# One 512-column matmul for the high and low part of the activations, with the sum of the two PSUM halves at the evacuation

## The chip, the cores and the metric

The kernel runs on one core of one Trainium2 chip. The metric is the device time of one execution, in microseconds (us); smaller is better. TensorE is PE in the rows (its weight loads are PEld), VectorE is DVE, ScalarE is ACT, GpSimd is POOL, SyncE is SP.

## The reference

One layer of a decoder trunk on 256 tokens of width 2048. Cut to what matters here:

```python
proj = x @ w_in                      # 256 x 2048 by 2048 x 15392
# split of the columns: lru_x, lru_y, gla_q, gla_k, gla_v, gla_r, dn_qkv, beta, a, dn_z, gate_logits
y_lru = rg_lru(lru_x, lru_y)         # causal conv of 4 taps, gates, scan
y_gla = gla(gla_q, gla_k, gla_v, gla_r)
y_dn  = gated_deltanet(dn_qkv, beta, a, dn_z)      # causal conv of 4 taps, silu, chunk recurrence
gates = sigmoid(gate_logits + b_gate)
m = (gates[0] * (y_lru @ w_branch[0]) + gates[1] * (y_gla @ w_branch[1])
     + gates[2] * (y_dn @ w_branch[2])) @ w_out
x1 = layernorm(alpha * x + m)
out = layernorm(alpha * x1 + square(relu(x1 @ w1 + b1)) @ w2 + b2)   # hidden width 8192
```

All inputs are float32.

## The kernel before, in words

Each float32 operand of a large product is split into a high part (`hi`, the value as float32r) and a low part (`lo`, the rest), by `split` (L93): a cast on ACT (L94) and a subtraction on DVE (L95). A product is then three matmuls: hi by hi, hi by lo, lo by hi.

Most of the products are channel tiles: `jobB` (L129) computes 128 output channels for all 256 tokens. The weights are stationary (a 128 x 128 tile of `hi` or `lo` for each slice of 128 of the contraction), the activations move with 256 columns (`xh`, `xl`; in the MLP `x1h`, `x1l`). `mmB` (L121) takes 8 slices: for each of them weight `hi` by `xh` (L124) and the same weight `hi` by `xl` (L125), then eight times weight `lo` by `xh` (L127). All add up in the first 256 columns of one PSUM tile (`accB`, 512 columns wide, four buffers). A job of 16 slices is 48 matmuls. There are 113 channel tiles in the mixers (the first four run in a loop of their own, L187 to L191, slice by slice as x arrives) and 64 in the first product of the MLP (the first three in a loop of their own, L1089 to L1094, with the transposes of x1).

`evac` of the job then takes the PSUM tile: a causal conv (L343: a scaled copy on ACT, three multiply-adds of 253 to 255 columns on DVE that read PSUM), a plain copy (L362), products with decays (L422, L430, L431), a silu (L434), a tanh for a gate (L864), or in the MLP relu and square, both on ACT (L1037, L1038).

The other products have the weights as the moving operand: GLA's values (L467 to L469) and the output projection (L915 to L917) with 512 columns and, in one quarter, 256, the second product of the MLP (L1199 to L1201) with 512 and 256. The branch projections (`job_branch`, L975) have weights stationary and 256 columns moving, as a channel tile has, with `yh` and `yl`.

What sets the order: `run_jobs` (L1002) walks the list of jobs; before it emits the matmuls of a job, it emits the load (1 MB by SP's queue, three buffers) and the split of the job after it (`hi` and `lo` have three buffers of 8 slices each). After a job, `pump` (L145) emits steps of the mixers (LRU, GLA, DeltaNet), up to about 2 us of DVE and 2.2 us of ACT work, whose small matmuls stand between the jobs on PE. The order on each engine is then fixed by the scheduler when the program is built, by priority and data dependence; at run time each engine takes its instructions in this order.

Of the kernel before, what the change touches and what calls it, by code (L numbers as in the profile page):

```python
# [25 lines left out]
# columns of the packed per-channel parameters  # L26
# [16 lines left out]
# columns of the packed constants  # L43
# [10 lines left out]
# columns of the parameters that are needed later  # L54
# [4 lines left out]
# rows of the small projections in their channel tile  # L59
# [6 lines left out]
def trunk_kernel(ctx, tc, xw, xtok, par, lat, con, wab, wa2, wB, wV, wBr, wO, w1, w2a, w2b, rows, out):  # L66
# [23 lines left out]
    def t1_tile(name, shape, dt=F32):  # L90
        return sm.tile(shape, dt, tag="t1", name=name, bufs=6)
# [6 lines left out]
    xh = [big.tile([P, 8, T], F32R, tag="xh", name=f"xh{i}", bufs=2) for i in range(2)]  # L98
    xl = [big.tile([P, 8, T], F32R, tag="xl", name=f"xl{i}", bufs=2) for i in range(2)]
# [29 lines left out]
    def jobB(src, evac, rh=None, rl=None):  # L129
        rh, rl = rh or xh, rl or xl  # L130
        job = Job(src, 8 * len(rh), None, None)

        def mm():
            acc = mm_tile("accB")
            n = len(rh)
            for i in range(n):
                mmB(acc[:, :T], job, rh[i], rl[i], i, i == 0, i == n - 1)
            evac(acc[:, :T])
# [24 lines left out]
    # ---- inputs that the first jobs need  # L163
    # x and the first four channel tiles together, one slice of the contraction at a time
# [11 lines left out]
    for k in range(KT):  # L176
# [56 lines left out]
    # ---- small projections: GLA's low rank, beta and decay of DeltaNet  # L233
# [9 lines left out]
    def evac_small(acc):  # L243
        ve.tensor_scalar(zs, acc, col(C_DTB), col(C_SGN), ALU.add, ALU.mult)
        live.append(gen_small())

    def gen_small():
        # GLA's log decay: 16 gk per head
# [47 lines left out]
        # beta, g: token rows  # L296
# [19 lines left out]
        # GLA: cumulated log decay in chunks of 64, and its exponentials  # L316
# [23 lines left out]
    # ---- LRU  # L340
# [10 lines left out]
    def evac_lru_x(k):  # L351
        def f(acc):
            if k % 4 == 0:
                lru["xc", k // 4] = b4_tile("xc", [P, 4, T])
            conv(acc, lru["xc", k // 4][:, k % 4, :], C_LRU_W + 4 * k, col(C_LRU_B + k))
# [11 lines left out]
    def gen_lru(hf):  # L367
# [14 lines left out]
        # gelu  # L382
# [32 lines left out]
    # ---- GLA  # L415
    gla = {}

    def evac_gla_q(h):
        def f(acc):
            if h == 0:  # L420
                gla["qe"] = b4_tile("qe", [P, 4, T])
            ve.scalar_tensor_tensor(gla["qe"][:, h, :], acc, P ** -0.5, gla["eb"][:, h, :], ALU.mult, ALU.mult)  # L422
        return f

    def evac_gla_k(h):
        def f(acc):
# [7 lines left out]
    def silu2(acc, dst, use_act=True):  # L434
        """dst = 2 silu(acc)"""
# [4 lines left out]
    def evac_gla_r(k):  # L440
        def f(acc):
            if k % 4 == 0:
                gla["r", k // 4] = b4_tile("rr", [P, 4, T])
            silu2(acc, gla["r", k // 4][:, k % 4, :])
# [164 lines left out]
    def evac_dn_z(k):  # L609
        def f(acc):  # L610
            if k % 4 == 0:
                dn["z"][k // 4] = b4_tile("dz", [P, 4, T])
            silu2(acc, dn["z"][k // 4][:, k % 4, :])
# [31 lines left out]
    def gen_dn():  # L645
# [6 lines left out]
        for tt in range(NT):  # L652
# [31 lines left out]
            # inverse of the unit upper triangle I + M, blocks of 32 by substitution  # L684
# [37 lines left out]
            # blocks of 64, then of 128: D - D N D  # L722
# [45 lines left out]
            # chunk recurrence  # L768
# [88 lines left out]
    # ---- gates and branches  # L857
# [31 lines left out]
    # ---- output projection, first norm  # L889
# [112 lines left out]
    def run_jobs(js, hooks=()):  # L1002
        """Jobs in order; the split of a job stands before the mixers' steps of the one before it."""
# [23 lines left out]
    # ---- MLP, first product  # L1027
    x1h = [big.tile([P, 8, T], F32R, tag="xh", name=f"x1h{i}", bufs=2) for i in range(2)]
    x1l = [big.tile([P, 8, T], F32R, tag="xl", name=f"x1l{i}", bufs=2) for i in range(2)]
    h = []  # L1030

    def evac_h(c):
        def f(acc):
# [3 lines left out]
            sc.activation(t, acc, AF.Relu, bias=col(C_B1 + c))  # L1037
            sc.activation(h[c // 4][:, c % 4, :], t, AF.Square)  # L1038
# [3 lines left out]
    js = [jobB(w1[c], evac_h(c), x1h, x1l) for c in range(FF // P)]  # L1042
# [19 lines left out]
    # ---- norm of the mixer, transposed for the MLP  # L1062
    mv = [norm_stats(tt) for tt in range(NT)]
    acc = [mm_tile("accH") for _ in range(G)]
    for q in range(4):
# [6 lines left out]
        for kp in range(2):  # L1072
# [271 lines left out]
```

## Time and profile before

| | |
|---|---|
| Time, three runs | 1744.10, 1744.58, 1745.21 us |
| Median | 1744.58 us |
| Span of the profiled execution | 1743.0 us (the page gives no other time of it) |
| PE busy | 1722.7 us, 99% of the span |
| DVE busy | 1058.2 us, 61% |
| ACT busy | 889.8 us, 51% |
| POOL busy | 76.7 us, 4% |
| Granted clock of PE, mean over the run | 0.997 |

The span goes from the first to the last instruction of the one profiled execution; the runs are timed without it. The median lies 1.6 us above the span. A busy PE says that matmuls were under way, not that they started as closely as they can: what one costs in a stream is read from the starts of its neighbours, since the duration of one (283 ns for 256 columns) goes on while the next have begun.

### The profile page before, as it was taken

The page shows a single profiled execution, that of the slowest core. Times are in us where ns is not written, and L with a number is a line of the kernel's source. Part 1 is how long each engine was busy: PE and PEld are TensorE (multiplying, and loading weights), DVE is VectorE, ACT ScalarE, POOL GpSimd, SP SyncE. Part 2 cuts the span into 40 slices and gives each one's busy share as a digit, 9 for nine tenths or more (in the row PEclk, how much of TensorE's full clock was granted, in tenths as well). Part 3 has the DMA queues.
Part 4 walks back from the last instruction along what each step waited for, and adds up shares of the span by engine and source line. Part 5 has one row for each costly group of instructions (what it writes and reads, how often), then busy time and mean ns, then how long its engine had stood idle before and what let it go on. Part 6 is the DMA issues. An engine that isn't in the chain of part 4 may idle for free.

```text
span 1743.0 us, 30261 instructions
## 1 busy us (share of the span) xinstructions
PE 1722.7 (99%) x12782; PEld 1644.9 (94%) x12782; DVE 1058.2 (61%) x1353; ACT 889.8 (51%) x1209; POOL 76.7 (4%) x112
## 2 busy tenths in 40 slices
PE   8999999999999999999999999999999999999997
PEld 8999898999999999999998899999999988888897
DVE  7876456876765585565555675444444455576767
ACT  6785445785344443444444455554545444455553
POOL 0000000000120203000000000000000000000000
PEclk9999999999999999999999999999999999999999
DMA  8445543444564446355566835555545455555552
GB/s 328 150 170 187 197 173 125 166 170 149 184 194 148 161 170 187 130 181 182 184 217 223 308 109 209 190 177 187 187 177 193 172 192 195 194 193 193 203 193 97
DMA packets 52536, 319.96 MB, mean 184 GB/s; under 512 B 6752, under 2 KB 7136, under 8 KB 18992
## 3 DMA queue, kind: packets, MB, share of 16 engines
q1 hardware_dynamic: 49280, 310.92, 50.3%
q0 software_dynamic: 2976, 6.84, 1.5%
q8 instruction: 100, 1.64, 0.4%
q14 instruction: 36, 0.29, 0.0%
q10 hardware_dynamic: 144, 0.26, 0.0%
HBM read 315.09 MB, written 2.88 MB: 182 GB/s over the span
## 4 chain that ended last, share of the span: by engine, by line
PE 97%; DVE 1%; DMA 1%; ACT 0%; issue 0%; SPq 0%; DVEq 0%
PE accB L124 19%; PE accB L127 19%; PE accB L125 19%; PE accM L1200 7%; PE accM L1201 7%; PE accM L1199 7%; PE accB L982 3%; PE accB L984 3%; PE accB L986 3%; PE accO L917 1%; PE accO L915 1%; PE accO L916 1%; PE accV L467 1%; PE accV L469 1%; PE accV L468 1%; DMA raw<-in_w_dram 0%
## 5 line engine op out<-in xcount | busy, mean ns | idle before, releaser
L95 DVE TENSOR_TENSOR lo<-raw,hi 128x1024 fp32r<-128x1024 f32 (+2 forms) x584 | 708.6, 1216 | 541.6 <-ACT hi L94 537.8
L94 ACT CAST hi<-raw 128x1024 fp32r<-128x1024 f32 (+2 forms) x584 | 602.4, 1034 | 757.1 <-PE accB L125 406.0
L124 PE MATMUL accB<-xh,hi 128*128 128x256 f32 x1744 | 431.0, 285 | 0.0
L125 PE MATMUL accB<-xl,hi 128*128 128x256 f32 x1744 | 427.9, 283 | 0.0
L124 PEld LDWEIGHTS accB<-xh,hi 128*128 128x128 f32 x1744 | 334.4, 192 | 2.4 <-issue 1.4
L125 PEld LDWEIGHTS accB<-xl,hi 128*128 128x128 f32 x1744 | 334.5, 192 | 0.4
L127 PE MATMUL accB<-xh,lo 128*128 128x256 f32 x1744 | 244.9, 283 | 0.0
L124 PE MATMUL accB<-x1h,hi 128*128 128x256 f32 x976 | 239.7, 283 | 0.0
L125 PE MATMUL accB<-x1l,hi 128*128 128x256 f32 x976 | 239.5, 283 | 0.0
L127 PEld LDWEIGHTS accB<-xh,lo 128*128 128x128 f32 x1744 | 225.0, 192 | 0.1
L1200 PE MATMUL accM<-hi,hl 128*128 128x512 f32 (+1 forms) x608 | 212.8, 350 | 0.0
L1199 PE MATMUL accM<-hi,hh 128*128 128x512 f32 (+1 forms) x608 | 212.8, 350 | 0.0
L1201 PE MATMUL accM<-lo,hh 128*128 128x512 f32 (+1 forms) x608 | 212.8, 350 | 0.0
L125 PEld LDWEIGHTS accB<-x1l,hi 128*128 128x128 f32 x976 | 187.4, 192 | 0.0
L124 PEld LDWEIGHTS accB<-x1h,hi 128*128 128x128 f32 x976 | 187.4, 192 | 0.0
L127 PE MATMUL accB<-x1h,lo 128*128 128x256 f32 x976 | 137.0, 283 | 0.0
L1199 PEld LDWEIGHTS accM<-hi,hh 128*128 128x128 f32 x608 | 115.1, 189 | 15.1
L1200 PEld LDWEIGHTS accM<-hi,hl 128*128 128x128 f32 x608 | 115.1, 189 | 15.0
L1201 PEld LDWEIGHTS accM<-lo,hh 128*128 128x128 f32 x608 | 115.1, 189 | 14.8
L127 PEld LDWEIGHTS accB<-x1h,lo 128*128 128x128 f32 x976 | 125.9, 192 | 0.0
L982 PE MATMUL accB<-yh,hi 128*128 128x256 f32 x384 | 109.8, 286 | 0.0
L986 PE MATMUL accB<-yh,lo 128*128 128x256 f32 x384 | 108.7, 283 | 0.0
(308 smaller groups left out, 1861.3 us busy)
## 6 DMA issues: line engine op xcount, KB each, us to landing
raw<-in_wB_dram SPq DMA_DIRECT2D x109, 1024.0 KB, 4.8
raw<-in_w_dram SPq DMA_DIRECT2D x64, 1024.0 KB, 4.8
raw<-in_w2a_dram SPq DMA_DIRECT2D x32, 1024.0 KB, 4.8
raw<-in_w2b_dram SPq DMA_DIRECT2D x32, 1024.0 KB, 4.8
raw<-in_wBr_dram SPq DMA_DIRECT2D x48, 512.0 KB, 3.4
raw<-in_wO_dram SPq DMA_DIRECT2D x16, 1024.0 KB, 4.9
raw<-in_wV_dram SPq DMA_DIRECT2D x8, 1024.0 KB, 4.8
raw<-in_xw_dram SPq DMA_DIRECT2D x15, 384.0 KB, 8.0
```

The lines of the kernel that those rows point to most:

```text
L94: i1 = sc.copy(hi, raw)
L95: i2 = ve.tensor_tensor(lo, raw, hi.bitcast(F32), ALU.subtract)
L124: te.matmul(acc, lhsT=hi[:, k, :], rhs=rh[:, k, :], start=start and k == 0, stop=False)
L125: te.matmul(acc, lhsT=hi[:, k, :], rhs=rl[:, k, :], start=False, stop=False)
L127: te.matmul(acc, lhsT=lo[:, k, :], rhs=rh[:, k, :], start=False, stop=stop and k == 7)
L467: te.matmul(accs[nh][tt], lhsT=sh, rhs=hi, start=k == 0, stop=False)
L982: te.matmul(acc[:, :T], lhsT=job.hi[0][:, 4 * i + k, :], rhs=yh[b][i][:, k, :], start=i == 0 and k == 0, stop=False)
L984: te.matmul(acc[:, :T], lhsT=job.hi[0][:, 4 * i + k, :], rhs=yl[b][i][:, k, :], start=False, stop=False)
L986: te.matmul(acc[:, :T], lhsT=job.lo[0][:, 4 * i + k, :], rhs=yh[b][i][:, k, :], start=False, stop=i == 1 and k == 3)
L1199: te.matmul(t, lhsT=sh, rhs=hi, start=k == 0, stop=False)
L1200: te.matmul(t, lhsT=sl, rhs=hi, start=False, stop=False)
L1201: te.matmul(t, lhsT=sh, rhs=lo, start=False, stop=k == NK2 - 1)
```

## The change

The activations' high and low part lie side by side, 256 and 256 columns for each slice (`xx`, made by `pairs`). The weight tile `hi` moves both as one matmul of 512 columns; weight `lo` moves the high part as before. The PSUM tile then holds hi by hi plus lo by hi in its first half and hi by lo in its second, and the evacuation adds the halves: `both` copies the second half to SBUF on ACT and adds the first half to it on DVE. The conv, the decays, the silu and the gate's tanh then read this sum in SBUF, no longer PSUM. In the MLP, the copy takes the bias with it, and relu and square become one instruction of DVE. The branch projections and the products with moving weights stay as they are. The pool of 256-column tiles (`t1`) has seven buffers in place of six.

```diff
+    def pairs(name):
+        t = [big.tile([P, 8, 2, T], F32R, tag="xx", name=f"{name}{i}", bufs=2) for i in range(2)]
+        return t, [v[:, :, 0, :] for v in t], [v[:, :, 1, :] for v in t]
+    xx, xh, xl = pairs("xx")
...
-    def mmB(acc, job, rh, rl, part, start, stop):
+    def mmB(acc, job, r, part, start, stop):
         hi, lo = job.hi[part], job.lo[part]
         for k in range(8):
-            te.matmul(acc, lhsT=hi[:, k, :], rhs=rh[:, k, :], start=start and k == 0, stop=False)
-            te.matmul(acc, lhsT=hi[:, k, :], rhs=rl[:, k, :], start=False, stop=False)
+            te.matmul(acc, lhsT=hi[:, k, :], rhs=flat(r[:, k]), start=start and k == 0, stop=False)
         for k in range(8):
-            te.matmul(acc, lhsT=lo[:, k, :], rhs=rh[:, k, :], start=False, stop=stop and k == 7)
+            te.matmul(acc[:, :T], lhsT=lo[:, k, :], rhs=r[:, k, 0, :], start=False, stop=stop and k == 7)
+
+    def both(acc, dst=None):
+        s = dst if dst is not None else t1_tile("sum", [P, T])
+        sc.copy(s, acc[:, T:])
+        ve.tensor_tensor(s, acc[:, :T], s, ALU.add)
+        return s
...
-            o = acc0[i][:, :T]
-            te.matmul(o, lhsT=h[:, i, :], rhs=kh, start=k == 0, stop=False)
-            te.matmul(o, lhsT=h[:, i, :], rhs=kl, start=False, stop=False)
-            te.matmul(o, lhsT=l[:, i, :], rhs=kh, start=False, stop=k == KT - 1)
+            te.matmul(acc0[i], lhsT=h[:, i, :], rhs=flat(xx[k // 8][:, k % 8]), start=k == 0, stop=False)
+            te.matmul(acc0[i][:, :T], lhsT=l[:, i, :], rhs=kh, start=False, stop=k == KT - 1)
...
-            conv(acc, c, C_DN_W + 4 * k)
+            conv(both(acc), c, C_DN_W + 4 * k)
...
-            sc.copy(lru["y", k // 4][:, k % 4, :], acc)
+            both(acc, lru["y", k // 4][:, k % 4, :])
...
             t = t1_tile("gate", [P, T])
-            sc.activation(t, acc, AF.Tanh, scale=0.5, bias=bgh[:, b * 16 + d:b * 16 + d + 1])
+            both(acc, t)
+            sc.activation(t, t, AF.Tanh, scale=0.5, bias=bgh[:, b * 16 + d:b * 16 + d + 1])
...
             t = t1_tile("hr", [P, T])
-            sc.activation(t, acc, AF.Relu, bias=col(C_B1 + c))
-            sc.activation(h[c // 4][:, c % 4, :], t, AF.Square)
+            sc.activation(t, acc[:, T:], AF.Identity, bias=col(C_B1 + c))
+            ve.tensor_tensor(t, acc[:, :T], t, ALU.add)
+            ve.scalar_tensor_tensor(h[c // 4][:, c % 4, :], t, 0.0, t, ALU.max, ALU.mult)
...
-                    r, o = x1h[k // 8][:, k % 8, :], acc[m][:, :T]
-                    te.matmul(o, lhsT=hi, rhs=r, start=k == 0, stop=False)
-                    te.matmul(o, lhsT=lo, rhs=r, start=False, stop=False)
-                    te.matmul(o, lhsT=hi, rhs=x1l[k // 8][:, k % 8, :], start=False, stop=k == KT - 1)
+                    te.matmul(acc[m], lhsT=hi, rhs=flat(xx1[k // 8][:, k % 8]), start=k == 0, stop=False)
+                    te.matmul(acc[m][:, :T], lhsT=lo, rhs=x1h[k // 8][:, k % 8, :], start=False, stop=k == KT - 1)
```

The order on the engines, at two places. On PE, the middle of a channel tile of the mixers before (`xh_75` and `xh_76` are the first and second eight slices of x):

```order
L124 MATMUL accB<-xh_75,hi 128x256
L125 MATMUL accB<-xl_77,hi 128x256
L127 MATMUL accB<-xh_75,lo 128x256 x8
L124 MATMUL accB<-xh_76,hi 128x256
L125 MATMUL accB<-xl_78,hi 128x256
```

Each `hi` tile is loaded and used twice, once for each half, before the eight of `lo` follow. On PE, the same place now, and the start of the next tile:

```order
L132 MATMUL accB<-xx_75,hi 128x512 x8
L134 MATMUL accB<-xx_75,lo 128x256 x8
L132 MATMUL accB<-xx_76,hi 128x512 x8
L134 MATMUL accB<-xx_76,lo 128x256 x8
L132 MATMUL accB<-xx_75,hi 128x512 x8
```

The pairs of L124 and L125 have become single matmuls of 512 columns; a tile is 32 matmuls in place of 48, of which 16 have 512 columns.

On ACT, at two of DeltaNet's channel tiles before (`cv` is the conv's result, `th` the tanh of the silu, `raw` the loaded weights):

```order
L345 ACTIVATE cv<-accB,pt 128x256
L94 CAST hi<-raw 128x1024
L437 ACTIVATE th<-cv 128x256
L94 CAST hi<-raw 128x1024
L345 ACTIVATE cv<-accB,pt 128x256
L437 ACTIVATE th<-cv 128x256
```

A tile's evacuation takes two instructions here, with casts of later weights around them. On ACT, the same two tiles now (`sum` is what `both` makes):

```order
L139 COPY sum<-accB 128x256
L94 CAST sqh<-sq 128x512
L94 CAST hi<-raw 128x1024
L357 ACTIVATE cv<-sum,pt 128x256
L94 CAST hi<-raw 128x1024
L450 ACTIVATE th<-cv 128x256
L139 COPY sum<-accB 128x256
L357 ACTIVATE cv<-sum,pt 128x256
L450 ACTIVATE th<-cv 128x256
```

One copy more stands in each tile, and casts of the next weights stand between the copy and the instruction that waits for DVE's sum in the first of them.

On DVE, at the second of these tiles before:

```order
L95 TENSOR_TENSOR lo<-raw,hi 128x1024
L438 SCALAR_TENSOR_TENSOR qk_3107<-th,cv 128x256
L95 TENSOR_TENSOR lo<-raw,hi 128x1024
L349 SCALAR_TENSOR_TENSOR cv<-accB,pt,cv 128x255
L349 SCALAR_TENSOR_TENSOR cv<-accB,pt,cv 128x254
L349 SCALAR_TENSOR_TENSOR cv<-accB,pt,cv 128x253
L438 SCALAR_TENSOR_TENSOR qk_3107<-th,cv 128x256
```

The conv's three instructions stand behind a subtraction of later weights and read `accB`. On DVE, the same tile now:

```order
L95 TENSOR_TENSOR lo<-raw,hi 128x1024
L451 SCALAR_TENSOR_TENSOR qk_2593<-th,cv 128x256
L140 TENSOR_TENSOR sum<-accB,sum 128x256
L361 SCALAR_TENSOR_TENSOR cv<-sum,pt,cv 128x255
L361 SCALAR_TENSOR_TENSOR cv<-sum,pt,cv 128x254
L361 SCALAR_TENSOR_TENSOR cv<-sum,pt,cv 128x253
L451 SCALAR_TENSOR_TENSOR qk_2593<-th,cv 128x256
```

The sum is one more instruction ahead of the conv, and the conv reads `sum` in place of `accB`.

## Rows read from the trace of the kernel before

**Rows 1.** Part 1 of the page: busy time, share and instructions of each engine.

```profile
PE 1722.7 (99%) x12782; PEld 1644.9 (94%) x12782; DVE 1058.2 (61%) x1353; ACT 889.8 (51%) x1209; POOL 76.7 (4%) x112
```

**Rows 2.** Part 4 of the page: the chain that ended last, by line.

```profile
PE accB L124 19%; PE accB L127 19%; PE accB L125 19%; PE accM L1200 7%; PE accM L1201 7%; PE accM L1199 7%; PE accB L982 3%; PE accB L984 3%; PE accB L986 3%; PE accO L917 1%; PE accO L915 1%; PE accO L916 1%; PE accV L467 1%; PE accV L469 1%; PE accV L468 1%; DMA raw<-in_w_dram 0%
```

**Rows 3.** Waits of the whole run: who <- whom, us in total, times, longest.

```profile
DVE lo L95 <- ACT hi L94: 537.8, 444, 2.6
ACT hi L94 <- PE accB L125: 406.0, 287, 3.0
```

**Rows 4.** Waits of PE alone: its two longest, same columns.

```profile
PE acc L189 <- ACT hi L94: 4.2, 2, 3.8
PE p_x L1077 <- DVE xt L1069: 2.0, 1, 2.0
```

**Rows 5.** Timeline of PE, 601 to 603 us: start, us, instruction. Fourteen rows left out.

```profile
601.05 0.28 PE L124 MATMUL accB<-xh,hi 128*128 128x256 f32 x1
...
602.85 0.28 PE L125 MATMUL accB<-xl,hi 128*128 128x256 f32 x1
```

**Rows 6.** Timeline of PE, 1599 to 1602 us, same columns. Eight rows left out.

```profile
1599.83 0.39 PE L1201 MATMUL accM<-lo,hh 128*128 128x512 f32 x1
...
1601.87 0.39 PE L1201 MATMUL accM<-lo,hh 128*128 128x512 f32 x1
```

**Rows 7.** Groups by line and shape, count | busy us, mean ns | idle: PE.

```profile
L124 PE MATMUL accB<-xh,hi 128*128 128x256 f32 x1744 | 431.0, 285 | 0.0
L124 PE MATMUL accB<-x1h,hi 128*128 128x256 f32 x976 | 239.7, 283 | 0.0
L189 PE MATMUL acc<-xh,hi 128*128 128x256 f32 x64 | 19.1, 298 | 4.2 <-ACT hi L94 4.2
L1092 PE MATMUL accH<-x1h,hi 128*128 128x256 f32 x48 | 14.1, 296 | 0.0
```

**Rows 8.** The same view: ACT and DVE on 256 columns, the prices.

```profile
L362 ACT COPY yb<-accB 128x256 f32<-128x256 f32 x8 | 2.9, 364 | 0.0
L430 DVE TENSOR_TENSOR ke<-accB,gr 128x256 f32<-128x256 f32 x4 | 1.7, 417 | 3.1 <-PE accB L127 3.1
L349 DVE SCALAR_TENSOR_TENSOR cv<-accB,pt,cv 128x255 f32<-128x255 f32 x24 | 11.4, 477 | 0.0
L438 DVE SCALAR_TENSOR_TENSOR qk<-th,cv 128x256 f32<-128x256 f32 x16 | 6.7, 421 | 5.3 <-ACT th L437 5.3
L1037 ACT ACTIVATE hr<-accB,pt 128x256 f32<-128x256 f32 x61 | 29.1, 477 | 0.0
L1038 ACT ACTIVATE h<-hr 128x256 f32<-128x256 f32 x64 | 26.7, 418 | 1.9
```

**Rows 9.** Stretches of 25 us: busy PE, PEld, DVE, ACT, POOL; clock; DMA share; GB/s.

```profile
325.00:350.00 25.00, 25.00 (x207) 24.80 (x206) 22.46 (x37) 18.58 (x30) 0.00 (x0) 1.00 0.49 171
350.00:375.00 25.00, 25.00 (x203) 24.68 (x202) 19.56 (x29) 20.14 (x31) 0.00 (x0) 1.00 0.52 178
625.00:650.00 25.00, 25.00 (x210) 25.00 (x210) 24.18 (x47) 9.91 (x11) 2.49 (x3) 1.00 0.43 152
1100.00:1125.00 25.00, 25.00 (x211) 25.00 (x210) 10.94 (x9) 13.21 (x19) 0.00 (x0) 1.00 0.54 188
```

**Rows 10.** Timeline of all engines: three splits, each with its first use on PE.

```profile
99.63 1.03 ACT L94 CAST hi<-raw 128x1024 fp32r<-128x1024 f32 x1
...
102.23 0.28 PE L124 MATMUL accB<-xh,hi 128*128 128x256 f32 x1
...
640.61 1.05 ACT L94 CAST hi<-raw 128x1024 fp32r<-128x1024 f32 x1 [1.83 <-PE accB L125]
...
647.13 0.28 PE L124 MATMUL accB<-xh,hi 128*128 128x256 f32 x1
...
647.25 1.21 DVE L95 TENSOR_TENSOR lo<-raw,hi 128x1024 fp32r<-128x1024 f32 x1
...
650.25 0.28 PE L986 MATMUL accB<-yh,lo 128*128 128x256 f32 x1
```

More of the change, by code (lines that the diff above doesn't have):

```diff
@@ L90, in t1_tile @@
     def t1_tile(name, shape, dt=F32):
-        return sm.tile(shape, dt, tag="t1", name=name, bufs=6)
+        return sm.tile(shape, dt, tag="t1", name=name, bufs=7)
     def split(raw, hi, lo):
@@ L119, in prep, with flat, jobB @@
             job.lo.append(lo)
-    def mmB(acc, job, rh, rl, part, start, stop):
+    def flat(v):
+        return v.rearrange("p a t -> p (a t)")
+    def mmB(acc, job, r, part, start, stop):
         hi, lo = job.hi[part], job.lo[part]
         for k in range(8):
-            te.matmul(acc, lhsT=hi[:, k, :], rhs=rh[:, k, :], start=start and k == 0, stop=False)
-            te.matmul(acc, lhsT=hi[:, k, :], rhs=rl[:, k, :], start=False, stop=False)
+            te.matmul(acc, lhsT=hi[:, k, :], rhs=flat(r[:, k]), start=start and k == 0, stop=False)
         for k in range(8):
-            te.matmul(acc, lhsT=lo[:, k, :], rhs=rh[:, k, :], start=False, stop=stop and k == 7)
-    def jobB(src, evac, rh=None, rl=None):
-        rh, rl = rh or xh, rl or xl
-        job = Job(src, 8 * len(rh), None, None)
+            te.matmul(acc[:, :T], lhsT=lo[:, k, :], rhs=r[:, k, 0, :], start=False, stop=stop and k == 7)
[4 more added lines that the diff above has]
+        return s
+    def jobB(src, evac, r=None):
+        r = r or xx
+        job = Job(src, 8 * len(r), None, None)
         def mm():
             acc = mm_tile("accB")
-            n = len(rh)
+            n = len(r)
             for i in range(n):
-                mmB(acc[:, :T], job, rh[i], rl[i], i, i == 0, i == n - 1)
-            evac(acc[:, :T])
+                mmB(acc, job, r[i], i, i == 0, i == n - 1)
+            evac(acc)
         job.mm = mm
@@ L243, in evac_small @@
     def evac_small(acc):
-        ve.tensor_scalar(zs, acc, col(C_DTB), col(C_SGN), ALU.add, ALU.mult)
+        ve.tensor_scalar(zs, both(acc), col(C_DTB), col(C_SGN), ALU.add, ALU.mult)
         live.append(gen_small())
@@ L354, in f @@
                 lru["xc", k // 4] = b4_tile("xc", [P, 4, T])
-            conv(acc, lru["xc", k // 4][:, k % 4, :], C_LRU_W + 4 * k, col(C_LRU_B + k))
+            conv(both(acc), lru["xc", k // 4][:, k % 4, :], C_LRU_W + 4 * k, col(C_LRU_B + k))
         return f
@@ L421, in f @@
                 gla["qe"] = b4_tile("qe", [P, 4, T])
-            ve.scalar_tensor_tensor(gla["qe"][:, h, :], acc, P ** -0.5, gla["eb"][:, h, :], ALU.mult, ALU.mult)
+            ve.scalar_tensor_tensor(gla["qe"][:, h, :], both(acc), P ** -0.5, gla["eb"][:, h, :], ALU.mult, ALU.mult)
         return f
@@ L429, in f @@
                 gla["kd"] = b4_tile("kd", [P, 4, T])
+            acc = both(acc)
             ve.tensor_tensor(gla["ke"][:, h, :], acc, gla["enb"][:, h, :], ALU.mult)
@@ L443, in f @@
                 gla["r", k // 4] = b4_tile("rr", [P, 4, T])
-            silu2(acc, gla["r", k // 4][:, k % 4, :])
+            silu2(both(acc), gla["r", k // 4][:, k % 4, :])
             if k == 7:
@@ L612, in f @@
                 dn["z"][k // 4] = b4_tile("dz", [P, 4, T])
-            silu2(acc, dn["z"][k // 4][:, k % 4, :])
+            silu2(both(acc), dn["z"][k // 4][:, k % 4, :])
         return f
@@ L950, in trunk_kernel @@
     jobs = []
-    evac_small(acc0[0][:, :T])
+    evac_small(acc0[0])
     for k in range(G0 - 1):
-        evac_lru_x(k)(acc0[1 + k][:, :T])
+        evac_lru_x(k)(acc0[1 + k])
     for hf in range(2):
@@ L1025, in before_out @@
                 nc.sync.dma_start(xt[tt, i], xtok[tt * P:(tt + 1) * P, i * 1024:(i + 1) * 1024])
-    x1h = [big.tile([P, 8, T], F32R, tag="xh", name=f"x1h{i}", bufs=2) for i in range(2)]
-    x1l = [big.tile([P, 8, T], F32R, tag="xl", name=f"x1l{i}", bufs=2) for i in range(2)]
+    xx1, x1h, x1l = pairs("xx1")
     h = []
@@ L1036, in f @@
             t = t1_tile("hr", [P, T])
-            sc.activation(t, acc, AF.Relu, bias=col(C_B1 + c))
-            sc.activation(h[c // 4][:, c % 4, :], t, AF.Square)
+            sc.activation(t, acc[:, T:], AF.Identity, bias=col(C_B1 + c))
+            ve.tensor_tensor(t, acc[:, :T], t, ALU.add)
+            ve.scalar_tensor_tensor(h[c // 4][:, c % 4, :], t, 0.0, t, ALU.max, ALU.mult)
         return f
     G = 3
-    js = [jobB(w1[c], evac_h(c), x1h, x1l) for c in range(FF // P)]
+    js = [jobB(w1[c], evac_h(c), xx1) for c in range(FF // P)]
     def prep_first():
@@ L1099, in trunk_kernel @@
     for a in range(G):
-        evac_h(a)(acc[a][:, :T])
+        evac_h(a)(acc[a])
     rb = {}
```

2 lines of the change are left out of this document (removed).

## Prediction, made before the changed kernel ran

> **What bounds the kernel now.** I read the busy shares first: PE is busy for 99% of the span, DVE for 61%, ACT for 51% [rows 1]. A busy PE is not yet a bound, so the chain that ended last comes next: it is PE's nearly everywhere, and the three lines of the channel tiles, L124, L125 and L127, hold 19% of the span each, 57% together [rows 2]. The waits say which way the dependence goes: ACT stood 406 us, 287 times, until PE had finished with a buffer of `hi`, and DVE 538 us for ACT's cast [rows 3], while PE's two longest waits are 4.2 us at the start and 2.0 us at the norm of the mixers [rows 4]. The engines that prepare the weights run ahead and are held back by PE. What shortens the stream on PE therefore shortens the run, as long as they stay ahead.
>
> What a matmul costs in the stream is the step from one start to the next. With 256 columns, 601.05 to 602.85 us holds 15 steps: 120.0 ns each [rows 5]. With 512 columns, 1599.83 to 1601.87 us holds 9 steps: 226.7 ns each [rows 6]. Both streams load a new weight tile for each matmul. At the higher of the two clocks, 2.4 GHz, which the rows of both kinds of stretch show as granted (1.00 in [rows 9]), 256 columns are 106.7 ns and 512 are 213.3 ns; both steps lie 13.3 ns above. So a matmul carries a fixed 13.3 ns beside its columns, and two of 256 columns pay it twice.
>
> **The change part by part.**
>
> *The pairs on PE.* Each L124 and its L125 take 2 x 120.0 = 240.0 ns; the one matmul in their place takes 226.7 ns. That is 13.3 ns for each pair. L124 counts 1744 and 976 [rows 7], together 2720 pairs: 2720 x 13.3 ns = **36.3 us**, all of it on the path, in tiles that go from 48 x 0.120 = 5.76 us to 16 x 0.2267 + 16 x 0.120 = 5.55 us. L127 stays as it is.
>
> *The two stages with their own loops.* L189 has 64 pairs (0.85 us), L1092 has 48 (0.64 us) [rows 7]. Here the activations are made just ahead of PE, and a 512-column matmul needs the low half before it starts, where the first matmul before needed the high half alone: about one DVE subtraction of 256 columns (0.42 us by the nearest rows, [rows 8]) once in each stage. The bounds are -1.5 us, if only PE counts, and +0.8 us, if nothing is won and both first matmuls start later. PE's wait on L189 is only 4.2 us [rows 4], so most of the stage goes by PE's pace: I take -1.0 us.
>
> *The sum of the halves in the mixers.* 113 tiles get a copy from PSUM on ACT and an addition on DVE that reads PSUM. The nearest rows of the same size are ACT's copy of `accB`, 0.364 us, and DVE's product with `accB`, 0.417 us [rows 8]. At the eight tiles that were copied anyway, ACT's is no addition. The conv's three instructions (0.477 us each, from PSUM) now read SBUF; the silu's last step, which has no PSUM operand, takes 0.421 us [rows 8], so they may give back 3 x 0.056 = 0.17 us a tile. I cost all this at nothing wherever ACT and DVE run ahead, and the cover is their lead over PE. I matched the splits with the jobs in order over the mixers. A typical one is ready 5.5 us ahead: a cast ends at 641.66 us and is used at 647.13. The tightest cast ends at 100.66 us, used at 102.23: 1.6 us. The tightest subtractions are where DeltaNet's inverse fills DVE: one ends at 648.46 us, used at 650.25: 1.8 us [rows 10]. If the cover is gone, a tile costs up to 0.364 + 0.417 = 0.78 us of PE's time.
>
> *Where it is nearly gone.* A stretch of 25 us holds at most 25 / 5.76 = 4.3 tiles, and PE will go through it in 25 - 4.3 x 0.21 = 24.1 us. From 325 to 350 us (DeltaNet's channel tiles) DVE has 22.46 us of work [rows 9]; with 4.3 x (0.417 - 0.17) = 1.1 us more it is 23.5 us. From 350 to 375 us ACT has 20.14 us [rows 9]; with 4.3 x 0.364 = 1.6 us it is 21.7 us. Both still fit, barely on DVE. From 625 to 650 us DVE has 24.18 us [rows 9], and three gates bring 1.25 us: 25.4 us in the 24.4 us that PE will need. It falls behind by 1.0 us, against a lead of 1.8 us. So the sums say no stall, or small ones. The sum adds two waits inside a tile: DVE's addition for ACT's copy, and the conv's scaled copy on ACT for DVE's addition. Behind these on their engines stand subtractions and casts of the next weights, for which PE waits in the end. I take **+2 us** for all such stalls, with 0 below and, above, the case of the 24 DeltaNet conv tiles (L349, count 24 in [rows 8]) fully uncovered: 24 x 0.78 = 19 us.
>
> *The MLP.* ACT loses the square (0.418 us) and keeps an instruction like L1037; DVE gains an addition (0.417 us) and a multiply from SBUF (0.421 us) a tile [rows 8]. From 1100 to 1125 us DVE has 10.94 us and ACT 13.21 us of work [rows 9]: DVE comes to about 14.5 us of 24. That cover is ample: 0 us.
>
> *The loads.* SP's queue brings the same bytes with the same three buffers; the DMA share is around 0.5 in these stretches [rows 9], and tiles that are 4% shorter raise it by 0.02: 0 us. The seventh `t1` buffer answers for the `sum` tile, which lives from the copy to the last read.
>
> *The sum.* -36.3 - 1.0 + 2 = -35.3 us. The profiled execution has a span of 1743.0 us, which becomes 1707.7; the median of the runs lies 1.6 us above the span, and the time becomes **1709 us**.
>
> [...]
>
> **The rivals.**
>
> *Late splits (0.17).* PE stays the bound, but the DeltaNet and LRU stages lose the lead, because copy, addition and conv wait for each other across two in-order queues that are 80 to 90% full. For it: DVE's 22.46 of 25 us [rows 9] and the tightest leads of 1.6 and 1.8 us [rows 10]. Against it: 287 waits of ACT for PE [rows 3]. It gives back 4 to 19 us: 1711 to 1726, around 1716.
>
> *The fixed cost hardly falls (0.05).* The second matmul of a pair uses the weights that the first has used, and may already hide part of its 13.3 ns; or the merged stream, which changes between 512 and 256 columns, runs at another step than the pure one. A pair would then save between nothing and half of 13.3 ns, 0 to 18 us in 2720 pairs, 9 us in the middle: 1736. Against it: in the stream of pairs first and second matmul have the same step, 120.0 ns on the mean of 15 [rows 5], and 512 columns are 226.7 [rows 6]. [...]
>
> *No change (0.03).* The 512-column matmul takes 240 ns in this loop, so nothing falls on PE, and no cover is lost: 1744 or 1745.
>
> *Slower (0.05).* The evacuation takes the place of PE as the bound: ACT's copy waits for the tile's last matmul, and the casts of the weights after next stand behind it. If the lead of 5.5 us is used up for good, each of the 109 mixer tiles that `jobB` runs (1744 / 16) starts 0.78 us later: +85 us against -37.3 us, or about 1792 us. It decides from 37.3 / 0.78 = 48 uncovered tiles on; below this the run is still faster. Against it: over the whole mixers ACT is nowhere near full for 48 tiles in a row, and it waits for PE far more than PE for it [rows 3, 4].
>
> **How the numbers follow.** The forecast, PE's 37.3 us less 0 to 4 us of stalls, has 0.70 and gives 1707 to 1711. The range must leave out no more than 2 in 10: with the late splits up to their upper bound it reaches 1726, and below I allow 2 us for a matmul step or a stage that does better than the rows, to 1705. Left out are the fixed cost (0.05), no change (0.03), slower (0.05). A measurement of this kernel can tell about 0.2%, or 3.5 us, from no change. Faster by more: 0.70 + 0.17 + 0.05 = 0.92; within it 0.03; slower 0.05.
>
> **What would show it.** In the profile after: starts of the `hi` matmuls 227 ns apart and of the `lo` ones 120 ns; a tile every 5.55 us in the MLP; L127's line unchanged at 120 ns. PE's waits stay below some 10 us in all; ACT still waits for PE to release `hi`, though for less. Late splits would show as PE waits on `hi` or `lo` between 50 and 160 us, 300 and 400 us, or around 640 us. The prediction is wrong in its first term if the 512-column step is not 227 ns, and in its second if PE waits more than 19 us for splits.

## The result, and the profile after

The changed kernel took 1721.4 us (median of four runs, 1719.63 to 1723.06) against 1744.34 us for the kernel before beside it: a ratio of 0.987, 95% interval 0.9856 to 0.9884. That is faster, by 23 us, and inside the range; the forecast of 1709 us was 12 us too low. In the profiled executions the span went from 1743.0 to 1720.4 us, 22.6 us less, where 37.3 us less had been counted on PE. So some 15 us are missing, and the question of this study is where they went. The two profiled executions also differ by the clock: in that of the kernel before, the mean granted clock was 0.57 from 1004 to 1008 us, at the norm of the mixers, which loses up to 1.7 us; in that of the change it was 1.00 there. Differences of spans are therefore not good to better than 1 or 2 us.

The page of the kernel after: busy shares, the chain that ended last by line, and the two groups of the channel tiles on PE (count | busy us, mean ns | idle).

```profile
PE 1695.8 (99%) x9950; PEld 1495.0 (87%) x9950; DVE 1141.8 (66%) x1594; ACT 899.0 (52%) x1250; POOL 76.6 (4%) x112
...
PE accB L132 36%; PE accB L134 18%; PE accM L1211 7%; PE accM L1213 7%; PE accM L1212 7%; PE accB L996 3%; PE accB L998 3%; PE accB L1000 3%; PE accO L931 1%; PE accO L930 1%; PE accO L929 1%; PE accV L480 1%; PE accV L482 1%; PE accV L481 1%; PE acc L202 1%; PE accH L1105 1%
...
L132 PE MATMUL accB<-xx,hi 128*128 128x512 f32 x2720 | 685.8, 394 | 0.3 <-ACT hi L94 0.3
...
L134 PE MATMUL accB<-xx,lo 128*128 128x256 f32 x2720 | 379.4, 282 | 0.4 <-DVE lo L95 0.4
```

PE is still busy for 99% of the span, as in [rows 1], with 2832 matmuls less: the 2720 pairs, and the 64 + 48 pairs of the two loops at the start of a stage. The two lines of the channel tiles hold 54% of the chain, where three held 57% [rows 2]. Their work waits for a split for 0.7 us in all. So the missing time is either in the steps of the stream or in waits elsewhere. The waits of PE, whole run (us in total, times, longest):

```profile
PE acc L202 <- ACT hi L94: 4.2, 1, 4.2
PE p_bg L315 <- DVE lr L311: 2.5, 1, 2.5
PE p_x L1091 <- DVE xt L1083: 2.0, 1, 2.0
...
PE p_v L615 <- DVE vc L451: 0.9, 1, 0.9
```

The first and the third are those of [rows 4]. New is the second, not a wait for a split at all: `p_bg`, the transposes of beta and decay in DeltaNet's gate chain, for `lr`. ACT still waits for PE to release a `hi`, for less than in [rows 3], as the lead got smaller:

```profile
ACT hi L94 <- PE accB L132: 341.9, 243, 3.4
```

**First place: the stream itself.** The timeline of PE after, 206 to 215 us, start and duration; a row holds eight matmuls.

```profile
206.32 1.98 PE L132 MATMUL accB<-xx,hi 128*128 128x512 f32 x8
208.13 1.11 PE L134 MATMUL accB<-xx,lo 128*128 128x256 f32 x8
209.09 2.00 PE L132 MATMUL accB<-xx,hi 128*128 128x512 f32 x8
210.93 1.12 PE L134 MATMUL accB<-xx,lo 128*128 128x256 f32 x8
211.88 2.00 PE L132 MATMUL accB<-xx,hi 128*128 128x512 f32 x8
```

Read the starts. The first eight follow a stream of 512 columns and take 208.13 - 206.32 = 1.81 us, 226 ns each, as counted. The second eight follow 256-column matmuls and take 1.84 us; so do all later ones. Matmul by matmul, where the rows merge eight, the eight steps are 233, 236, 228, 232, 231, 227, 227, 227 ns, and the eight of 256 columns behind them 113, 119 and six times 120. A run of eight and eight takes 2793 ns where 8 x 226.7 + 8 x 120.0 = 2773 was counted: 20 ns. There are 340 such runs (2720 / 8), so **6.8 us** of the 36.3 are lost here.

**Second place: one stretch at the start.** 50 to 70 us and three pieces of it: busy PE, PEld, DVE, ACT, POOL; clock; DMA share; GB/s.

```profile
50.00:70.00 20.00, 16.67 (x85) 13.79 (x85) 13.78 (x25) 15.39 (x20) 0.00 (x0) 0.91 0.36 122
...
62.00:64.00 2.00, 0.00 (x0) 0.00 (x0) 1.97 (x5) 2.00 (x3) 0.00 (x0) 0.93 0.86 360
64.00:66.00 2.00, 1.91 (x6) 1.62 (x7) 1.97 (x3) 0.46 (x2) 0.00 (x0) 0.50 0.00 0
66.00:68.00 2.00, 2.00 (x10) 1.62 (x9) 2.00 (x6) 0.15 (x1) 0.00 (x0) 0.72 0.00 0
```

PE idles for 3.3 us of the 20, of which one gap of 2.55 us covers all of 62 to 64 us, and behind it the granted clock is at the lower level, 1.2 GHz (0.50), and comes back before 68 us; at a mean of 0.91 the 20 us lose up to 1.8 us more. Together some **5 us**. What PE waits for is in the timeline of all engines (an `ACT_TABLE_LOAD` gets ACT the table of the function that follows).

```profile
47.42 1.28 ACT L295 ACT_TABLE_LOAD   x1
49.15 1.28 ACT L297 ACT_TABLE_LOAD   x1
51.82 1.28 ACT L295 ACT_TABLE_LOAD   x1
53.60 1.28 ACT L297 ACT_TABLE_LOAD   x1
55.12 1.28 ACT L295 ACT_TABLE_LOAD   x1
58.43 1.28 ACT L297 ACT_TABLE_LOAD   x1
59.73 1.06 ACT L297 ACTIVATE gr<-gu 128x1024 f32<-128x1024 f32 x1
60.82 1.23 DVE L300 TENSOR_TENSOR ge<-ge,gr 128x1024 f32<-128x1024 f32 x1 [0.81 <-ACT gr L297]
62.02 0.42 DVE L140 TENSOR_TENSOR yb<-accB,yb 128x256 f32<-128x256 f32 x1
62.37 1.22 DVE L301 TENSOR_TENSOR gu<-gu,ge 128x1024 f32<-128x1024 f32 x1
63.69 0.34 DVE L311 TENSOR_SCALAR lr<-lz,acol 32x256 f32<-32x256 f32 x1
64.09 0.69 PE L315 MATMUL p_bg<-ct,lr 128*128 128x128 f32 x2 [2.55 <-DVE lr L311]
```

The gate chain takes a Ln (L295) and an Exp (L297) of three tiles (`lu`, `lw`, `gu`). The program gives all Ln first, but the scheduler built another order around the added sums: Ln, Exp, Ln, Exp, Ln, Exp. ACT loads a table before each, six times 1.28 us; before there were four such loads. The last Exp, `gr`, ends at 60.79 us; DVE, in its order, stands at `ge` for it, then has a sum of the new kind (L140) and `gu`, and only then `lr`, for which PE's transposes wait. That is a second change of order: in the kernel before, `lr` stood right behind `ge`, ahead of `gu`.

```profile
56.72 0.34 DVE L299 TENSOR_SCALAR lr<-lz,acol 32x256 f32<-32x256 f32 x1
57.09 1.23 DVE L289 TENSOR_TENSOR gu<-gu,ge 128x1024 f32<-128x1024 f32 x1
```

There `ge` ends at 56.69 us and `lr` starts at 56.72; now they are 62.05 and 63.69, and the sum and `gu` between them cost 1.6 us. The Trainium skill says of this load, in "ScalarE: Activation LUTs", section "What ACT_TABLE_LOAD costs", that it takes about 1283 ns and a drain of 1380 ns besides. The rows agree with the first part; of the second nothing shows here, since the cast before a load ends at 58.41 us, the load starts at 58.43 and `gr` at 59.73, 1.30 us later.

The theory at this point: the missing time is the 20 ns at each change from 256 to 512 columns, 6.8 us, and the late gate chain, 5 to 6 us, and the sums cost next to nothing otherwise. The rivals: the sums cost their time all over the mixers (late splits); the pairs gain less than 13.3 ns in the steady stream too.

### The profile page after: what moved, and what is told of

It reads as the page before. It is cut to its first block, busy times and chain, and to the rows that moved or that the text cites. A ratio compares the mean times of both kernels' runs of the same rounds, so it can differ in the third digit from the quotient of the medians.

```text
span 1720.4 us, 24923 instructions
## 1 busy us (share of the span) xinstructions
PE 1695.8 (99%) x9950; PEld 1495.0 (87%) x9950; DVE 1141.8 (66%) x1594; ACT 899.0 (52%) x1250; POOL 76.6 (4%) x112
## 3 DMA queue, kind: packets, MB, share of 16 engines
q8 instruction: 78, 1.28, 0.3%
## 4 chain that ended last, share of the span: by engine, by line
PE 96%; DVE 2%; ACT 1%; DMA 1%; issue 0%; SPq 0%; DVEq 0%; ACTq 0%
PE accB L132 36%; PE accB L134 18%; PE accM L1211 7%; PE accM L1213 7%; PE accM L1212 7%; PE accB L996 3%; PE accB L998 3%; PE accB L1000 3%; PE accO L931 1%; PE accO L930 1%; PE accO L929 1%; PE accV L480 1%; PE accV L482 1%; PE accV L481 1%; PE acc L202 1%; PE accH L1105 1%
## 5 line engine op out<-in xcount | busy, mean ns | idle before, releaser
L132 PE MATMUL accB<-xx,hi 128*128 128x512 f32 x2720 | 685.8, 394 | 0.3 <-ACT hi L94 0.3
L132 PEld LDWEIGHTS accB<-xx,hi 128*128 128x128 f32 x2720 | 490.6, 189 | 90.8 <-issue 1.4
L134 PEld LDWEIGHTS accB<-xx,lo 128*128 128x128 f32 x2720 | 370.9, 190 | 27.7 <-DVE lo L95 1.2
L134 PE MATMUL accB<-xx,lo 128*128 128x256 f32 x2720 | 379.4, 282 | 0.4 <-DVE lo L95 0.4
L998 PE MATMUL accB<-yl,hi 128*128 128x256 f32 x384 | 108.9, 284 | 0.0
L996 PEld LDWEIGHTS accB<-yh,hi 128*128 128x128 f32 x384 | 73.6, 192 | 0.4
L998 PEld LDWEIGHTS accB<-yl,hi 128*128 128x128 f32 x384 | 73.6, 192 | 0.2
L1000 PEld LDWEIGHTS accB<-yh,lo 128*128 128x128 f32 x384 | 73.6, 192 | 0.0
L95 DVE TENSOR_TENSOR hl<-h,hh 128x512 fp32r<-128x512 f32 (+1 forms) x94 | 65.1, 695 | 0.0
L94 ACT CAST hh<-h 128x512 fp32r<-128x512 f32 (+1 forms) x94 | 58.7, 627 | 0.0
```

What stands on the lines that cost most here:

```text
L94: i1 = sc.copy(hi, raw)
L95: i2 = ve.tensor_tensor(lo, raw, hi.bitcast(F32), ALU.subtract)
L132: te.matmul(acc, lhsT=hi[:, k, :], rhs=flat(r[:, k]), start=start and k == 0, stop=False)
L134: te.matmul(acc[:, :T], lhsT=lo[:, k, :], rhs=r[:, k, 0, :], start=False, stop=stop and k == 7)
L996: te.matmul(acc[:, :T], lhsT=job.hi[0][:, 4 * i + k, :], rhs=yh[b][i][:, k, :], start=i == 0 and k == 0, stop=False)
L998: te.matmul(acc[:, :T], lhsT=job.hi[0][:, 4 * i + k, :], rhs=yl[b][i][:, k, :], start=False, stop=False)
```

## The experiments

In the diffs the changed kernel has the minus. The kernel before, run beside them, had medians of 1743.4, 1744.42 and 1743.85 us in the three groups of runs.

**Without the sums.** The evacuations read the first half alone, in the mixers and in the MLP.

```diff
...
-            evac(acc)
+            evac(acc[:, :T])     # both() then hands it on, with no addition
...
```

> This kernel leaves the addition of the second PSUM half out (the low part of the activations is lost), so the evacuations are those of the kernel before, on the changed stream of matmuls. Theory: about 7.6 us of the missing gain lies in the stream (512-column steps of 233, 236, 228, 232, 231 ns after every eight of 256 columns, 20 ns a run of sixteen) and stays; about 6.5 us are waits at 50 to 75 us that the copy and addition bring, and go. Then 1714 to 1716 us. Rival: the evacuations hold all 14 us that are missing: 1707 to 1709 us. Rival: the evacuations cost nothing and all of it is in the stream: 1721 us.

1714.83 us (1713.71 to 1715.67), ratio 0.9832 (0.9819 to 0.9846). All sums together are worth 6.6 us against the change, not the whole 12 us: late splits all over are ruled out as the only cause, and what is left over the forecast of 1709 us is about the 6.8 us of the stream. But the scheduler also gave this kernel four table loads, so it took away two suspects at once. The runs below go after them one by one.

**Sixteen high slices, then sixteen low ones.** A tile then changes from 256 to 512 columns once, not twice.

```diff
...
             for i in range(n):
-                mmB(acc, job, r[i], i, i == 0, i == n - 1)
+                for k in range(8):
+                    te.matmul(acc, lhsT=job.hi[i][:, k, :], rhs=flat(r[i][:, k]), ...)
+            for i in range(n):
+                for k in range(8):
+                    te.matmul(acc[:, :T], lhsT=job.lo[i][:, k, :], rhs=r[i][:, k, 0, :], ...)
...
```

> All sixteen matmuls of hi (512 columns), then all sixteen of lo (256 columns), in a tile. Theory: the longer 512-column steps come from the change from 256 to 512 columns, which each tile then makes once in place of twice: slices 9 to 16 step at 226.7 ns, and 170 changes less by 20 ns give 3.4 us, 1718 us. If the scheduler's new order also removes the table loads on ACT at 47 to 60 us (two in place of six), up to 5 us more, 1713 us; this part is to be read apart, in the stretch 50 to 75 us. Rival: the longer steps belong to the first five slices of each half of x by their place in memory: then slices 9 to 13 show 233, 236, 228, 232, 231 again and the stream gains nothing.

1713.76 us (1712.18 to 1716.58), ratio 0.9828 (0.9815 to 0.9842). Its timeline of PE in the MLP:

```profile
1246.76 2.08 PE L155 MATMUL accB<-xx,lo 128*128 128x256 f32 x16
1248.67 3.82 PE L152 MATMUL accB<-xx,hi 128*128 128x512 f32 x16
1252.32 0.88 PE L155 MATMUL accB<-xx,lo 128*128 128x256 f32 x6
```

The sixteen high slices take 1252.32 - 1248.67 = 3.65 us, some 20 ns over 16 x 226.7 = 3627: the five late steps stand at the head of the group, and slices 9 to 16 step at 227 ns. So what costs is the change of width, once for each group, and not the position in an eight. A tile takes 5.567 us, 20 ns less than the change's, 3.4 us over 170 tiles. This order too has only two table loads, so its time holds both gains. PE waits for `lr` again, though, for 0.5 us (the same wait is shown below for the run with both corrections).

**The change in the MLP's first product alone.** The mixers keep their three matmuls of 256 columns and their evacuation.

```diff
...
+        if not job.wide:                  # wide: the MLP's jobs alone
+            for k in range(8):
+                te.matmul(acc[:, :T], lhsT=hi[:, k, :], rhs=r[:, k, 0, :], ...)
+                te.matmul(acc[:, :T], lhsT=hi[:, k, :], rhs=r[:, k, 1, :], ...)
+            for k in range(8):
+                te.matmul(acc[:, :T], lhsT=lo[:, k, :], rhs=r[:, k, 0, :], ...)
+            return
...
```

> The change in the MLP's first product alone, the mixers as before. Theory: 976 pairs by 13.3 ns less 122 changes by 20 ns, 13.0 - 2.4 = 10.6 us, about half a us more from the three tiles beside the transposes, and no new wait: 1733 to 1734 us. Rival (the added work on DVE costs time in the MLP too): 1737 us or more. Rival (nothing but the pairs counts): 1731 us.

1733.53 us (1731.01 to 1735.23), ratio 0.9936 (0.9922 to 0.995). With 5.587 us a tile (two runs of 2793 to 2794 ns) against 5.76, 61 tiles give 10.6 us and the 48 pairs of the loop some 0.3 us: 1743.4 - 10.9 = 1732.5 us. The run is within 1 us of that, and its executions scatter from 1731 to 1735 us: the MLP has the gain of its steps and no other loss that can be seen, which fits its cover of ACT and DVE.

**Two table loads.** The three Exp are held behind the three Ln by an order given to the scheduler; nothing else is changed.

```diff
-        for z, e, u, r in sets:
-            sc.activation(u, u, AF.Ln)
-        for z, e, u, r in sets:
-            sc.activation(r, u, AF.Exp, scale=-1.0)
+        lns = [sc.activation(u, u, AF.Ln) for z, e, u, r in sets]
+        with ExitStack() as behind:
+            for i in lns:
+                behind.enter_context(tc.issue_after(i.ins))
+            for z, e, u, r in sets:
+                sc.activation(r, u, AF.Exp, scale=-1.0)
```

> The changed kernel with one edge in the order: in the small chain of beta and decay, the exponentials on ACT stand behind all three logarithms, so two table loads in place of six between 40 and 65 us. Theory: the six loads (1.28 us each, four in the kernel before) carry the chain that PE waits for at 64 us; the 2.5 us wait, the half clock after it and the split waits before it go, and the time is 1716 to 1718 us. Rival (DVE's added work makes the chain late, not the loads): the wait stays, 1720 to 1722 us.

1715.64 us (1715.12 to 1718.05), ratio 0.984 (0.9827 to 0.9853): just under the 1716 to 1718 us that were expected, 5.8 us under the change, with all sums in it, and within 1 us of the kernel without sums. In the profiled executions the stretch from the first `accB` of the jobs to the first of GLA's values (`accV`) goes from 162.77 - 30.01 = 132.8 us in the change to 156.59 - 29.31 = 127.3 us here: 5.5 us, so nearly all of the difference lies in it. Its timeline of all engines (the two loads, `lr`, the transposes):

```profile
46.75 1.28 ACT L294 ACT_TABLE_LOAD   x1
50.92 1.28 ACT L299 ACT_TABLE_LOAD   x1
58.14 0.35 DVE L313 TENSOR_SCALAR lr<-lz,acol 32x256 f32<-32x256 f32 x1
59.39 0.38 PE L317 MATMUL p_bg<-ct,lr 128*128 128x128 f32 x2
```

`lr` is there 0.9 us before PE comes to it, and the stretch has no idle PE and no lower clock:

```profile
50.00:70.00 20.00, 20.00 (x115) 17.65 (x115) 18.40 (x30) 13.33 (x18) 0.00 (x0) 1.00 0.56 207
```

**Six loads without sums, six loads in the kernel before, and a control.** The opposite order was given to the scheduler, the six loads of the change in its sequence, in three kernels: the one without sums, the kernel before, and the change itself.

```diff
+        behind = None
+        for z, e, u, r in sets[1:] + sets[:1]:
+            with ExitStack() as st:
+                if behind is not None:
+                    st.enter_context(tc.issue_after(behind.ins))
+                ln = sc.activation(u, u, AF.Ln)
+            with tc.issue_after(ln.ins):
+                behind = sc.activation(r, u, AF.Exp, scale=-1.0)
```

> The run without the addition of the halves (the low part of the activations is left out), with the six table loads of the change put back in its order. If the six loads alone make the gate chain late, 1718 to 1721 us (1714.8 us without them, up to 6 more). If it takes the loads and the sums together, 1714.8 to 1716 us.

> The kernel before with six table loads in the gate chain in place of its four, in the order of the change. If the loads alone make the chain late, TensorE waits at the transposes of beta and decay near 60 us and the time is 2 to 6 us over the kernel before, 1745 to 1749 us. If the lead of the old tiles (5.76 us each) covers two more loads of 1.28 us, no change: 1743 to 1744 us and no wait there.

> A control for the run with two table loads: the changed kernel with the order of Ln and Exp fixed by the same kind of edit, but in the order that gives six loads. If the six loads, together with the sums of the halves, make the gate chain late, the wait of TensorE at the transposes of beta and decay is there again (about 2.5 us, with the clock at half behind it) and the time is that of the change, 1720 to 1723 us. If the run with two loads was faster for another reason (the other order that the edit led to), 1715 to 1717 us.

Without sums: 1716.37 us (1715.11 to 1718.12), ratio 0.9842 (0.9829 to 0.9856), just over the 1714.8 to 1716 us of the second case and well under the first. The kernel before with six loads: 1744.47 us beside 1744.42, ratio 1.0001 (0.9992 to 1.001), no change. The control: 1722.07 us (1720.24 to 1725.24), ratio 0.9877 (0.9863 to 0.9892), the time of the change, with its wait:

```profile
PE p_bg L319 <- DVE lr L315: 2.6, 1, 2.6
```

What became of the lead, the time from the end of `lr` to the transposes that read it, is in the timelines. Without sums, four loads:

```profile
57.11 0.34 DVE L315 TENSOR_SCALAR lr<-lz,acol 32x256 f32<-32x256 f32 x1
60.69 0.38 PE L319 MATMUL p_bg<-ct,lr 128*128 128x128 f32 x2
```

Without sums, six loads:

```profile
60.96 0.34 DVE L319 TENSOR_SCALAR lr<-lz,acol 32x256 f32<-32x256 f32 x1
61.72 0.38 PE L323 MATMUL p_bg<-ct,lr 128*128 128x128 f32 x2
```

The kernel before, six loads:

```profile
58.30 0.35 DVE L303 TENSOR_SCALAR lr<-lz,acol 32x256 f32<-32x256 f32 x1
60.48 0.38 PE L307 MATMUL p_bg<-ct,lr 128*128 128x128 f32 x2
```

Together (the kernel before by the rows above, with its transposes at 60.69 us):

| kernel | sums | table loads | lead of `lr` over PE | time, us |
|---|---|---|---|---|
| without sums | no | 4 | 60.69 - 57.45 = 3.2 us | 1714.8 |
| without sums, six loads | no | 6 | 61.72 - 61.30 = 0.4 us | 1716.4 |
| change, two loads | yes | 2 | 59.39 - 58.49 = 0.9 us | 1715.6 |
| change | yes | 6 | none, PE waits 2.55 us | 1721.4 |
| control | yes | 6 | none, PE waits 2.6 us | 1722.1 |
| before | no | 4 | 60.69 - 57.06 = 3.6 us | 1744.3 |
| before, six loads | no | 6 | 60.48 - 58.65 = 1.8 us | 1744.5 |

Two loads more take 2.8 us of lead without sums (3.2 to 0.4) and 1.8 us in the kernel before (3.6 to 1.8), and in neither does PE wait: "the table loads alone" falls. With six loads, the sums turn 0.4 us of lead into 2.55 us of waiting, 3.0 us, of which 1.6 us are the place of `lr` behind the sum and `gu`; with two loads, in the change's own order of matmuls, the sums make no wait either. The case between, the sums with the four loads of the kernel before, was not run. By these prices, as an estimate, 3.2 - 3.0 = 0.2 us of lead would be left, so "the sums alone" is not ruled out for the loss of the lead; what is shown is that taking loads away gives the 5.8 us back, and that the six loads do harm only where the sums are.

**Low slice right behind its high slice.** With two table loads, the width changes at every matmul.

```diff
         for k in range(8):
             te.matmul(acc, lhsT=hi[:, k, :], rhs=flat(r[:, k]), ...)
-        for k in range(8):
             te.matmul(acc[:, :T], lhsT=lo[:, k, :], rhs=r[:, k, 0, :], ...)
...
```

> The change with the low slice right behind its high slice, so that the stream changes width at every matmul, and with two table loads. Theory, priced from the loop of the first four tiles, which already alternates (233 to 236 ns for the step of 512 columns and 117 for that of 256, 353 ns a pair where 346.7 were counted): 6.3 ns x 2720 = 17 us of lost time in place of the 6.8 us in groups of eight, so some 10 us over the 1715.6 us of the run with two table loads, 1726 us. Rival 1 (every change from 256 to 512 costs the whole 20 ns that a group of eight loses): 2720 x 20 ns = 54 us, 1763 us. Rival 2 (the late steps belong to the start of a slice's group, not to the change of width): 1715.6 us.

1722.56 us (1720.1 to 1725.95), ratio 0.9878 (0.9864 to 0.9892): some 7 us over the two-load run, nearer to the theory's 10 than to either rival. But the steps don't bear the theory out. Its timeline of PE, two starts ten pairs apart at two places in the mixers, then in the MLP two starts nineteen pairs apart.

```profile
140.06 0.39 PE L132 MATMUL accB<-xx,hi 128*128 128x512 f32 x1
...
143.53 0.39 PE L132 MATMUL accB<-xx,hi 128*128 128x512 f32 x1
...
349.99 0.40 PE L132 MATMUL accB<-xx,hi 128*128 128x512 f32 x1
...
353.53 0.40 PE L132 MATMUL accB<-xx,hi 128*128 128x512 f32 x1
...
1245.95 0.39 PE L132 MATMUL accB<-xx,hi 128*128 128x512 f32 x1
...
1252.54 0.39 PE L132 MATMUL accB<-xx,hi 128*128 128x512 f32 x1
```

At the second place ten pairs take 3.54 us, 354 ns each, as priced. At the first they take 3.47 us, 347 ns each, and in the MLP nineteen take 6.59 us, 346.8 ns each: nothing is lost at all, with the same instructions. So the theory's price of 6.3 ns for each change is not a constant; there are two patterns, most of the mixers' tiles fell into the bad one and all the MLP's into the good one. Summed over the steps of all the jobs' tiles, this run loses 7.8 us in the mixers and nothing in the MLP against the counted steps, the two-load run 4.1 and 2.4: 1.2 us more, not 10. The rest of the longer time is not in the steps: in the profiled executions the first tile of the jobs starts 1.6 us later (30.87 against 29.31 us, from run to run), and PE waits 1.7 us for splits in the jobs, most of it near 62 us, and 1.0 us more at the output projection. That the time came near the theory is luck.

**Both corrections, and a mixture.** Sixteen and sixteen with two loads, and the same with alternating slices in the MLP, to use the good pattern there.

```diff
...
+                    if alternate:                      # the MLP's jobs
+                        te.matmul(acc[:, :T], lhsT=job.lo[i][:, k, :], rhs=r[i][:, k, 0, :], ...)
...
```

> Both corrections at once: all 16 high slices of a tile ahead of its 16 low ones, and no Exp of the gate chain ahead of the three Ln (two table loads in place of six). Theory (each change from 256 to 512 columns costs 20 ns of TensorE, and a tile has now one in place of two): 170 x 20 ns = 3.4 us under the 1715.6 us that the run without the extra table loads took, so 1712 us. Rival (the late steps behind a change of width are made up for elsewhere and cost the end nothing): 1715.6 us. The run with 16 slices a group took 1713.8 us with two loads already, so anything from 1711 to 1714 us leaves the theory standing.

> A candidate for the fastest: two table loads; in the mixers the 16 high slices of a tile ahead of its 16 low ones, which took 5.567 us a tile in the trace; in the first product of the MLP each low slice right behind its high one, which took 5.547 us a tile there and 5.650 us in the mixers. If a pair costs the counted 346.7 ns there again, the trace shows 230 and 117 ns by turns in the MLP, and the 64 tiles lose 20 ns less each than in the run with both corrections: 1.3 us under its 1715.5 us, 1714 us, which is within what the runs scatter. If the mixers' 353 ns come along, 64 x 83 ns = 5.3 us more, 1721 us.

Both corrections: 1715.52 us (1712.61 to 1716.86), ratio 0.9836 (0.9822 to 0.9849). That is the rival's 1715.6 us, and outside the 1711 to 1714 us that were to leave the theory standing. By the time alone the 3.4 us cannot be found; they are no more than the scatter of the runs. The trace shows where they went. From the first matmul of the MLP (`accH`) to the first of its second product (`accM`) it takes 1345.73 - 987.75 = 357.98 us, the two-load run 1347.43 - 988.26 = 359.17: 1.2 us less, as 61 changes of 20 ns are. From `accV` to the first of the output projection (`accO`) it is 735.2 against 737.1 us, 1.9 us less. But the new order gives some of it back: from the first tile of the jobs to `accV` it takes 128.2 us against 127.3, with a wait for `lr` that the two-load run has not, and at the output projection a wait of 1.3 us stands in place of 0.4.

```profile
PE p_bg L322 <- DVE lr L318: 0.5, 1, 0.5
```

The mixture: 1721.26 us (1720.35 to 1721.86), ratio 0.9872 (0.9856 to 0.9888). Its timeline of PE in the MLP, two starts seven pairs apart:

```profile
1250.09 0.40 PE L153 MATMUL accB<-xx,hi 128*128 128x512 f32 x1
...
1252.56 0.40 PE L153 MATMUL accB<-xx,hi 128*128 128x512 f32 x1
```

Seven pairs in 2.47 us, 353 ns each: the bad pattern, in the place where the run with alternating slices had the good one. That is the second case of what was expected, and its 1721 us. The mixture differs from the run with both corrections in the MLP alone, and is 5.7 us slower where the steps count 64 x 83 ns = 5.3 us: here what the steps lose does come through in the time. Which pattern an alternating stream takes is not set by its place or its instructions alone; what sets it was not found.

## Why the prediction was right or wrong

- **What bounds the kernel: right.** PE's stream does, and the time fell with it. The clock of the 512-column row, 1599 to 1602 us, which [rows 9] doesn't hold, was 1.00 too, as the prediction took it.
- **The pairs on PE: right in the mechanism, too large in size.** "2720 x 13.3 ns = 36.3 us" took the steps from streams of one width [rows 5, 6] for a stream of both. The change's own stream loses 20 ns in each run of eight and eight, 2.5 of the 13.3 ns a pair: 36.3 - 6.8 = 29.5 us; the run with two table loads, which has no other large loss, gained 1743.4 - 1715.6 = 27.8 us. By the prediction's own sign, a 512-column step that is not 227 ns, this term was wrong: five of eight take 228 to 236. The rival that named "another step than the pure one" for the merged stream had the mechanism, at a small part of its price.
- **The two loops: right.** An alternating pair takes 353 ns in place of three times 120; 112 pairs give 0.8 us, 1.0 was taken, and PE's wait of 4.2 us at the first is what it was.
- **The sums in the mixers: right in the places it looked at, wrong in the one it didn't.** At 325 to 375 us and near 640 us nothing stalls. The "+2 us for all such stalls" became 5 to 6 us before 70 us alone, and 0.9 us at `p_v`. The cover there was not the lead of the splits but that of the gate chain over the transposes, and the addition changed the scheduler's order, on ACT, which cost two table loads, and on DVE, where `lr` went behind the sum and `gu`. That a change of one operation reorders others on its engine was in the order of the changed program, before any run. The give-back of 0.17 us in the conv didn't come: L361 reads SBUF and takes 480 ns where L349 read PSUM and took 477 [rows 8].
- **The MLP and the loads: right.** The change there alone gave what its steps give. From 1100 to 1125 us DVE has 14.07 us of work (about 14.5 was worked out) and ACT 10.84.
- **The sum.** Of the 14.7 us by which the span fell short of 37.3 us, 6.8 are the widths and 5.5 the gate chain. From `accV` to `accO` the change takes 737.1 us and the kernel without sums 735.7 us, in one profiled execution each: the sums cost some 1.4 us there, of which 0.9 is the wait at `p_v`. The loops are 0.2. The rest, about 1 us, is less than what the clock and the start move between two executions, and stays open.
- **The range: held, in part by luck.** The case that was given 0.70, 1707 to 1711 us, did not come. 1721.4 us lies in the range because the range was drawn up to 1726 us for late splits, and that mechanism is not what happened: PE waited 0.7 us for splits in the channel tiles. Two other losses, widths and gate chain, took their place.

## What to carry to other kernels

Price a matmul in the stream in which it will stand: steps read from streams of one width missed what the change of width cost here, 20 ns a group, so groups of sixteen lost half of what groups of eight lost. When work is added to an engine that has room on average, look in the new order at what it does to that engine's table loads and to the shortest lead of every chain that PE waits for, not only of the weights. Where Ln and Exp of several tiles stand together, fix their order, so that the scheduler can't interleave them.

## What the runs showed of the hardware that was not expected

- A matmul of 512 columns behind a stream of 256-column ones steps at 228 to 236 ns for the first five, then at 227; the first two of 256 columns behind it take 113 and 119 ns instead of 120. Net 20 ns for a group, whether it has 8 or 16 slices.
- An alternating stream of the same instructions ran at 346.8 ns a pair in one kernel's MLP, at 353 ns in another's, and at 347 and 354 ns at two places of one kernel's mixers. What selects stays open.
- The conv's multiply-add on DVE took the same time from SBUF as from PSUM, 480 and 477 ns.
- The idle PE of 62 to 64 us was followed by more loss: the granted clock was 0.50, 1.2 GHz, from 64 to 66 us, and 0.72 on the mean of the 2 us after. Behind the wait of 1.1 us in the run with alternating slices the clock stayed at 1.00.
